# Half of x laid out by feature and loaded first over two queues, in a two-layer decoder trunk

## The chip, the core and the metric

The kernel runs on one core of one Trainium2 chip. The metric is the device time of one execution in microseconds (us), the median of several runs. The engines are named as the profile names them: PE (TensorE, the matrix engine; PEld is its weight load), ACT (ScalarE), DVE (VectorE), POOL (GpSimd) and SP (SyncE, which here only issues DMAs).

## What is computed

A trunk of two pre-norm residual layers with 256 positions and a width of 2048, in float32. Layer 0 is sliding-window attention with sinks, layer 1 attention in three branches. Each layer takes `h = rmsnorm(x)`, projects it (`h @ w_in`), attends, multiplies by a SiLU gate, projects again (`@ w_out`) and adds the result to x. A last rmsnorm ends it. What matters here is the start of layer 0:

```python
def rmsnorm(x, g):
    y = xf * lax.rsqrt(jnp.mean(xf * xf, axis=-1, keepdims=True) + NORM_EPS)
    return (y * g.astype(jnp.float32)).astype(x.dtype)
...
proj = h @ w_in
q, k, v, z = jnp.split(proj, ...)
q = apply_rope(q..., cos, sin); k = apply_rope(k..., cos, sin)
```

The cosines and sines come from `positions`, an input of 256 integers.

## The kernel before

To keep float32 precision in the products, each weight tile and each activation tile is split into a high part (`w_hi`, `hT[...,0,:]`, a rounded copy made on ACT) and a low part (the rest, a subtraction on DVE), and three products per K-tile (high x high, low x high, high x low) go into one PSUM bank. A K-tile is 128 of the 2048 features; there are 16, and the 256 positions are two halves t of 128 rows.

The work is a list of steps. A step loads 512 KB of weights into a tile `raw` (four buffers; `load`), splits it (`split`, three buffers of `w_hi` and `w_lo`; steps 0 and 1 in two halves) and runs its products (`half(0)` for t = 0, `half(1)` for t = 1, six products of 512 columns each). Eight steps fill two of three accumulator banks (`acc`); then `post` evacuates them. The first eight steps are the key and value columns of layer 0, called the first block below; its `post_kv` scales by `r = 1/rms`, which so is needed only there, copies k on ACT and v on DVE, and turns k by the rope tables on POOL.

The products need x by feature: `hT_pair(0, hT0, j)` transposes K-tiles 2j and 2j+1 on PE (four transposes), copies them times the norm's weight `gT` to the high part (ACT) and makes the low part (DVE). Pair 0 comes before the first step, and step i makes pair i+1. `first_block` (line 861) also computes, in steps 4 to 7, the squares of x, 512 columns at a time (`square`, on ACT with a running sum), and in step 7 `scales(0)`: a sum and two small operations on DVE, a power on POOL, then rq and rh on DVE, and `scale_rows`, which spreads rh over the columns with two transposes (`rbc`).

Loads are issued in this order on SP (lines 380 to 390 and 1283 to 1290): the identity matrix with the rope frequencies (`cst`), the norm weights (`nw`), x columns 0 to 511 (two halves), raw[0], x columns 512 to 1023, raw[1], the rest of x between raw[2] and raw[3]. POOL's software queue loads the positions and the sinks. PE bridges the wait with nine products of zeros (`idle`). The norm weights are transposed on PE (`nwT`) to get `gT`; the rope tables are made at once on DVE and ACT.

No instruction runs where it stands in the text. Every operation is recorded (line 217 is the one line that all of them show in the profile), with a price from `_price` (line 160 on). `Plan.order` (line 247) then runs a simulation with these prices: an engine that is free takes, of the operations that can start, the one with the lowest number, where the splits are moved ahead of everything and the products behind everything:

```python
heapq.heappush(able[e], (i - ops[i].early, i))
...
dma_free = max(dma_free, end + 700) + op.bytes / self.BYTES_NS
```

The result is a fixed order for each engine, which the chip follows first in, first out. An entry in `op.order` only forces this order in the plan; an entry in `op.deps` is a real dependence. In the plan a DMA issue costs SP and ACT 60 ns, a dependence into PE has 800 ns of slack, and a power on POOL costs some 500 ns.

Of the kernel before, what the change touches and what calls it, by code (L numbers as in the profile page):

```python
# [163 lines left out]
def _price(eng, method, args, kw, out, ins):  # L164
# [12 lines left out]
    if method == "dma_start":  # L177
        return (1050 if eng == "POOL" else 60, 2200)
    ptrs = sum(isinstance(kw.get(k), View) for k in ("scale", "bias", "scalar", "scalar1"))
# [159 lines left out]
@with_exitstack  # L339
def trunk(ctx: ExitStack, tc: tile.TileContext, x, positions, norm_w, final_norm_w,  # L340
          a_w_in, a_sinks, a_w_out, b_w_in, kc_pos, kc_w1, kc_w2, vc_pos, vc_w1, vc_w2,
          b_w_out, consts, out):
    nc = tc.nc
# [16 lines left out]
    def dram(ap, off, pattern):  # L360
        return bass.AP(tensor=ap.tensor, offset=ap.offset + off, ap=pattern)

    def copy(out, in_, scale=1.0):
        ACT.activation(out, in_, AF.Copy, scale=scale)

# [6 lines left out]
    ps = s_bank("idle")  # L372
    for _ in range(9):
        PE.matmul(ps, idle[:, 0:P], idle, start=True, stop=True)


    pos_i = sb.tile([P, NT], I32, name="pos_i")
    POOL.dma_start(pos_i, dram(positions, 0, [[1, P], [P, NT]]))
    cst = sb.tile([P, P + 8], F32, name="cst")
    SP.dma_start(cst, dram(consts, 0, [[CW, P], [1, P + 8]]))  # L380
    ident = cst[:, 0:P]
    nw = sb.tile([32, 512], F32, tag="q32", name="nw", bufs=2)[:, 0:P]
    SP.dma_start(nw, dram(norm_w, 0, [[P, 32], [1, P]]))
    xt = [sb.tile([P, D], F32, name=f"x{t}") for t in range(NT)]

    def load_x(j):
        for t in range(NT):
            SP.dma_start(xt[t][:, j * NB:(j + 1) * NB], dram(x, t * P * D + j * NB, [[D, P], [1, NB]]))

    load_x(0)  # L390
    sinks = sb.tile([P, 32], F32, name="sinks")
    POOL.dma_start(sinks, dram(a_sinks, 0, [[0, P], [1, 32]]))

    identr = sb.tile([P, P], F32R, name="identr")
    DVE.tensor_copy(identr, ident)
    nhalf = sb.tile([P, 1], F32, name="nhalf")
    DVE.memset(nhalf, -0.5)


    posf = sb.tile([P, NT], F32, name="posf")  # L400
    DVE.tensor_copy(posf, pos_i)
    ang = sb.tile([P, NT, 8], F32, name="ang")
    for t in range(NT):
        DVE.tensor_scalar(ang[:, t], cst[:, P:P + 8], posf[:, t:t + 1], None, op0=OP.mult)
    red = sb.tile([P, 2, NT, 8], F32, name="red")
    rnd = sb.tile([P, 2, NT, 8], F32, name="rnd")
    for i, shift in enumerate((0.0, 0.25)):
        DVE.tensor_scalar(rnd[:, i], ang, 1.0 / (2.0 * math.pi), shift, op0=OP.mult, op1=OP.add)
        DVE.tensor_scalar(rnd[:, i], rnd[:, i], MAGIC, None, op0=OP.add)
        DVE.tensor_scalar(rnd[:, i], rnd[:, i], -MAGIC, None, op0=OP.add)  # L410
        src = ang
        for c in TWO_PI:
            DVE.scalar_tensor_tensor(red[:, i], rnd[:, i], -c, src, op0=OP.mult, op1=OP.add)
            src = red[:, i]
        if i:
            DVE.tensor_scalar(red[:, i], red[:, i], math.pi / 2, None, op0=OP.add)
    lim = float(np.nextafter(np.float32(math.pi), np.float32(0)))
    DVE.tensor_scalar(red, red, lim, -lim, op0=OP.min, op1=OP.max)
    cs = sb.tile([P, NT, 2, 8], F32, name="cs")
    sn = sb.tile([P, NT, 2, 8], F32, name="sn")  # L420
    ACT.activation(sn[:, :, 1, :], red[:, 0], AF.Sin)
    ACT.activation(cs[:, :, 0, :], red[:, 1], AF.Sin)
    DVE.tensor_copy(cs[:, :, 1, :], cs[:, :, 0, :])
    DVE.tensor_scalar(sn[:, :, 0, :], sn[:, :, 1, :], -1.0, None, op0=OP.mult)

# [21 lines left out]
    mflat = mask.rearrange("p a b -> p (a b)")  # L447
    nsink = sb.tile([P, 32], F32, name="nsink")
    DVE.tensor_scalar(nsink, sinks, -1.0, None, op0=OP.mult)

    gT = sb.tile([P, 32], F32, name="gT")
    tb = t_bank("nwT")
    PE.transpose(tb[:, 0, 0:32], nw, ident[0:32, 0:32])
    copy(gT, tb[:, 0, 0:32])


# [66 lines left out]
    def hT_pair(i, hT, j):  # L523

        tb = t_bank("xT")
        for k in range(2):
            for t in range(NT):
                PE.transpose(tb[:, 2 * k + t, :], xt[t][:, (2 * j + k) * P:(2 * j + k + 1) * P], ident)
        src = [tb[:, 2 * k:2 * k + 2, :].rearrange("p a b -> p (a b)") for k in range(2)]
        g = [gT[:, i * KT + 2 * j + k:i * KT + 2 * j + k + 1] for k in range(2)]  # L530
        hi = [hT[:, 2 * j + k, 0, :] for k in range(2)]
        for k in range(2):
            copy(hi[k], src[k], scale=g[k])
        for k in range(2):
            DVE.scalar_tensor_tensor(hT[:, 2 * j + k, 1, :], src[k], g[k], hi[k].bitcast(F32),
                                     op0=OP.mult, op1=OP.subtract)
# [324 lines left out]
    def first_block(i):  # L861
        if i not in first_done:
# [431 lines left out]
    for i, st in enumerate(steps):  # L1294
# [23 lines left out]
def _consts():  # L1318
# [10 lines left out]
    for g in range(NG):  # L1329
# [25 lines left out]
```

## Time and profile before

| | |
|---|---|
| median of 3 runs | 793.22 us (792.34 to 793.55) |
| the profiled execution | 793.6 us, of which its span (first to last instruction) 791.5 |
| mean granted clock of PE | 0.99 |
| busy: PE, DVE, ACT, POOL | 775.1, 562.3, 466.0, 122.9 us |
| DMA | 128.77 MB, mean 163 GB/s |

Busy times of PE are modelled at their ends, so a busy PE is not always PE at its peak. The granted clock is 1.00 at 2.4 GHz and 0.50 at 1.2 GHz. In a timeline, a row is one instruction or several alike in a row; in the chain of waits, each piece is followed back from the last instruction to what released it.

### The profile page before, as it was taken

The page shows a single profiled execution, that of the slowest core. Times are in us where ns is not written, and L with a number is a line of the kernel's source. Part 1 is how long each engine was busy: PE and PEld are TensorE (multiplying, and loading weights), DVE is VectorE, ACT ScalarE, POOL GpSimd, SP SyncE. Part 2 cuts the span into 40 slices and gives each one's busy share as a digit, 9 for nine tenths or more (in the row PEclk, how much of TensorE's full clock was granted, in tenths as well). Part 3 has the DMA queues.
Part 4 walks back from the last instruction along what each step waited for, and adds up shares of the span by engine and source line. Part 5 has one row for each costly group of instructions (what it writes and reads, how often), then busy time and mean ns, then how long its engine had stood idle before and what let it go on. Part 6 is the DMA issues. An engine that isn't in the chain of part 4 may idle for free.

```text
span 791.5 us, 11613 instructions
## 1 busy us (share of the span) xinstructions
PE 775.1 (98%) x4004; PEld 625.8 (79%) x4004; DVE 562.3 (71%) x1164; ACT 466.0 (59%) x941; POOL 122.9 (16%) x169
## 2 busy tenths in 40 slices
PE   7999999999999999999999999999999999999995
PEld 4888878788788788888878887777868768768884
DVE  5657959859779655556756479869949878965562
ACT  6646647557466445554746477567648657744452
POOL 2102311213023000020101021111121131111110
PEclk7999999999999999999999999999999999999998
DMA  8555454554553555565667654434434453354652
GB/s 275 183 186 159 136 186 133 185 161 139 168 173 133 186 185 184 182 191 176 192 216 221 182 160 123 144 109 133 133 107 123 147 147 117 108 186 162 196 174 107
DMA packets 85995, 128.77 MB, mean 163 GB/s; under 512 B 6178, under 2 KB 43265, under 8 KB 85808
## 3 DMA queue, kind: packets, MB, share of 16 engines
q1 hardware_dynamic: 85536, 126.72, 50.5%
q0 software_dynamic: 400, 1.30, 0.6%
q8 instruction: 32, 0.52, 0.3%
q14 instruction: 27, 0.22, 0.1%
HBM read 125.91 MB, written 2.10 MB: 162 GB/s over the span
## 4 chain that ended last, share of the span: by engine, by line
PE 88%; DVE 5%; issue 3%; ACT 1%; DMA 1%; POOL 1%; SPq 0%; ACTq 0%; POOLq 0%; DVEq 0%
PE acc L217 72%; PE pv L217 5%; PE s L217 4%; PE pT L217 4%; DVE sm L217 2%; DVE w_lo L217 1%; PE qT L217 1%; PE xT L217 1%; DMA raw<-in_a_w_in 1%; DVE u L217 1%; ACT w_hi L217 1%; PE gates L217 1%; PE pcT L217 0%; POOL rope L217 0%; PE mlp L217 0%
## 5 line engine op out<-in xcount | busy, mean ns | idle before, releaser
L217 DVE TENSOR_TENSOR w_lo<-raw,w_hi 128x1024 fp32r<-128x1024 f32 (+1 forms) x231 | 293.1, 1271 | 166.0 <-ACT w_hi L217 160.5
L217 ACT ACTIVATE w_hi<-raw 128x1024 fp32r<-128x1024 f32 (+1 forms) x231 | 241.5, 1049 | 193.5 <-PE acc L217 157.3
L217 PE MATMUL acc<-w_hi,hT 128*128 128x512 f32 x768 | 247.1, 398 | 1.1 <-ACT w_hi L217 0.6
L217 PE MATMUL acc<-hT,w_hi 128*128 128x512 f32 x512 | 186.1, 398 | 0.0
L217 PEld LDWEIGHTS acc<-w_hi,hT 128*128 128x128 f32 x768 | 142.6, 190 | 33.4 <-ACT w_hi L217 3.5
L217 PE MATMUL acc<-w_lo,hT 128*128 128x512 f32 x384 | 151.9, 396 | 0.0
L217 PE MATMUL acc<-hT,w_lo 128*128 128x256 f32 x512 | 145.0, 285 | 0.0
L217 PEld LDWEIGHTS acc<-hT,w_hi 128*128 128x128 f32 x512 | 96.2, 188 | 21.9 <-issue 4.1
L217 PEld LDWEIGHTS acc<-hT,w_lo 128*128 128x128 f32 x512 | 96.7, 189 | 1.5 <-issue 0.8
L217 PE MATMUL acc<-w_hi,aT_lo 128*128 128x512 f32 x236 | 92.4, 391 | 0.0
L217 PE MATMUL acc<-w_hi,aT_hi 128*128 128x512 f32 x236 | 92.1, 392 | 0.0
L217 PE MATMUL acc<-w_lo,aT_hi 128*128 128x512 f32 x236 | 92.0, 391 | 0.0
L217 PEld LDWEIGHTS acc<-w_lo,hT 128*128 128x128 f32 x384 | 72.7, 189 | 16.4 <-issue 2.4
L217 ACT ACTIVATE sm<-sm,nmb 128x128 f32<-128x128 f32 (+1 forms) x128 | 56.8, 445 | 17.9 <-DVE nmb L217 15.7
L217 PEld LDWEIGHTS acc<-w_lo,aT_hi 128*128 128x128 f32 x236 | 44.3, 188 | 11.3 <-issue 2.4
L217 PEld LDWEIGHTS acc<-w_hi,aT_hi 128*128 128x128 f32 x236 | 44.3, 188 | 9.7 <-ACT w_hi L217 0.8
L217 PEld LDWEIGHTS acc<-w_hi,aT_lo 128*128 128x128 f32 x236 | 44.3, 188 | 8.9
L217 POOL TENSOR_TENSOR sm<-sm,denb 128x512 f32<-128x512 f32 (+1 forms) x16 | 29.1, 1818 | 140.7 <-DVE denb L217 82.0
L217 DVE CUSTOM_DVE_ANT_0 sm<-s,mask 128x128 f32<-128x128 f32 (+1 forms) x128 | 43.6, 348 | 9.2 <-PE s L217 8.9
L217 PEld LDWEIGHTS pT<-cst,sm 128*128 128x128 f32 x256 | 30.0, 140 | 13.8 <-issue 5.4
L217 PE MATMUL pT<-cst,sm 128*128 128x128 f32 x256 | 38.8, 276 | 1.2 <-DVE sm L217 0.8
L217 PE MATMUL s<-kTB,qT 128*128 128x272 f32 x192 | 37.8, 292 | 0.0
(187 smaller groups left out, 862.3 us busy)
## 6 DMA issues: line engine op xcount, KB each, us to landing
raw<-in_b_w_in SPq DMA_DIRECT2D x88, 512.0 KB, 3.6
raw<-in_a_w_in SPq DMA_DIRECT2D x72, 512.0 KB, 3.5
raw<-in_a_w_out SPq DMA_DIRECT2D x32, 512.0 KB, 3.5
raw<-in_b_w_out SPq DMA_DIRECT2D x32, 512.0 KB, 4.3
x<-in_x SPq DMA_DIRECT2D x8, 256.0 KB, 6.9
raw<-in_b_cmp_k_w SPq DMA_DIRECT2D x4, 512.0 KB, 3.7
raw<-in_b_cmp_v_w SPq DMA_DIRECT2D x4, 512.0 KB, 4.0
out<-x SPq DMA_DIRECT2D x4, 512.0 KB, 3.5
```

Of the source, the lines that this page charges most:

```text
L217: return getattr(eng.real, method)(*[real(a) for a in args], **{k: real(a) for k, a in kw.items()})
```

## The change

Two inputs are new, made on the host: `small` (128 x 74: the norm weights by feature, the sinks, the positions and the rope frequencies, spread over the partitions) and `xT` (K-tiles 0 to 7 of x by feature, 1 MB, so that two K-tiles are 2 KB in a row for each partition). Of x nothing is dropped: it is still loaded whole, but later. ACT issues the loads of `small` and of raw[0], in two halves of 256 KB; SP issues xT, two K-tiles at a time, three loads ahead of raw[1] and the fourth behind it. Pairs 0 to 3 read xT (`xf`) and need no transposes. x columns 1024 to 1535 are loaded ahead of raw[4], then 1536 to 2047 behind raw[4], 0 to 511 behind raw[5], 512 to 1023 behind raw[6]. The squares follow this order of columns, each pair behind a split in the plan; the rope tables and nsink stand in step 5. POOL makes the identity, and issues no load at the start. There is one idle product more, and an issue costs 450 ns in the plan. The core of the diff:

```diff
--- before.py
+++ after.py
...
             return (max(n, 256) / 2.4 + 2, 0)
         return (n * (4 if out.shape[0] > 64 else 2) / 2.4 + 2, 0)
     if method == "dma_start":
-        return (1050 if eng == "POOL" else 60, 2200)
+        return (1050 if eng == "POOL" else 450, 2200)
     ptrs = sum(isinstance(kw.get(k), View) for k in ("scale", "bias", "scalar", "scalar1"))
     ptrs += sum(isinstance(a, View) and math.prod(a.shape[1:]) == 1 and n > 2 for a in args[1:])
     psum = any(v.base.psum for v in ins)
...
     idle = sb.tile([P, NB], BF16, name="idle")
...
     DVE.memset(warm, 0.0)
     ACT.activation(warm, warm, AF.Sin)
     ps = s_bank("idle")
-    for _ in range(9):
+    for _ in range(10):
         PE.matmul(ps, idle[:, 0:P], idle, start=True, stop=True)
-    pos_i = sb.tile([P, NT], I32, name="pos_i")
-    POOL.dma_start(pos_i, dram(positions, 0, [[1, P], [P, NT]]))
-    cst = sb.tile([P, P + 8], F32, name="cst")
-    SP.dma_start(cst, dram(consts, 0, [[CW, P], [1, P + 8]]))
-    ident = cst[:, 0:P]
-    nw = sb.tile([32, 512], F32, tag="q32", name="nw", bufs=2)[:, 0:P]
-    SP.dma_start(nw, dram(norm_w, 0, [[P, 32], [1, P]]))
+    small_t = sb.tile([P, SMALL], F32, name="small")
+    ACT.dma_start(small_t, small)
+    gT = small_t[:, 0:32]
+    sinks = small_t[:, 32:64]
+    pos_i = small_t[:, 64:66].bitcast(I32)
+    inv_freq = small_t[:, 66:74]
     xt = [sb.tile([P, D], F32, name=f"x{t}") for t in range(NT)]
-    def load_x(j):
+    xf = sb.tile([P, KT, S], F32, tag="aT_hi", name="xf")
+    def load_x(j, later=None):
         for t in range(NT):
-            SP.dma_start(xt[t][:, j * NB:(j + 1) * NB], dram(x, t * P * D + j * NB, [[D, P], [1, NB]]))
-    load_x(0)
-    sinks = sb.tile([P, 32], F32, name="sinks")
-    POOL.dma_start(sinks, dram(a_sinks, 0, [[0, P], [1, 32]]))
+            op = SP.dma_start(xt[t][:, j * NB:(j + 1) * NB], dram(x, t * P * D + j * NB, [[D, P], [1, NB]]))
+            if later:
+                op.order.add(later.i)
+    def load_xf(k0, k1):
+        SP.dma_start(xf[:, k0:k1, :], dram(xT, k0 * S, [[XT * S, P], [S, k1 - k0], [1, S]]))
+    for k in range(0, 6, 2):
+        load_xf(k, k + 2)
+    ident = sb.tile([P, P], F32, name="ident")
+    POOL.memset(ident, 1.0)
+    for sign in (1, -1):
+        POOL.affine_select(out=ident, in_=ident, pattern=[[-sign, P]], compare_op=OP.is_ge, fill=0.0,
+                           base=0, channel_multiplier=sign)
     identr = sb.tile([P, P], F32R, name="identr")
     DVE.tensor_copy(identr, ident)
     nhalf = sb.tile([P, 1], F32, name="nhalf")
     DVE.memset(nhalf, -0.5)
...
     cs = sb.tile([P, NT, 2, 8], F32, name="cs")
     sn = sb.tile([P, NT, 2, 8], F32, name="sn")
+    def rope_tables(later):
+        DVE.tensor_scalar(nsink, sinks, -1.0, None, op0=OP.mult).order.add(later.i)
+        posf = sb.tile([P, NT], F32, name="posf")
+        DVE.tensor_copy(posf, pos_i).order.add(later.i)
...
         POOL.affine_select(out=mask_c[:, t], in_=mask_c[:, t], pattern=[[-16, 16]],
                            compare_op=OP.is_ge, fill=NEG, base=P * t - 31, channel_multiplier=1)
     mflat = mask.rearrange("p a b -> p (a b)")
-    nsink = sb.tile([P, 32], F32, name="nsink")
-    DVE.tensor_scalar(nsink, sinks, -1.0, None, op0=OP.mult)
-    gT = sb.tile([P, 32], F32, name="gT")
-    tb = t_bank("nwT")
-    PE.transpose(tb[:, 0, 0:32], nw, ident[0:32, 0:32])
-    copy(gT, tb[:, 0, 0:32])
     urgent, queue = deque(), deque()
     state = {"credit": 0.0, "rate": 0.0}
...
     def square(i, t, j):
         junk = sb.tile([P, NB], F32, tag="q32", name="junk", bufs=2)
-        ACT.activation(junk, xt[t][:, j * NB:(j + 1) * NB], AF.Square, accum_out=ssq[i][:, t, j:j + 1])
+        return ACT.activation(junk, xt[t][:, j * NB:(j + 1) * NB], AF.Square, accum_out=ssq[i][:, t, j:j + 1])
     def rstd(i, ts=slice(0, NT)):
         ms = sb.tile([P, NT], F32, tag="ms", name="ms", bufs=2)[:, ts]
...
     def hT_pair(i, hT, j):
-        tb = t_bank("xT")
-        for k in range(2):
-            for t in range(NT):
-                PE.transpose(tb[:, 2 * k + t, :], xt[t][:, (2 * j + k) * P:(2 * j + k + 1) * P], ident)
-        src = [tb[:, 2 * k:2 * k + 2, :].rearrange("p a b -> p (a b)") for k in range(2)]
+        if i == 0 and 2 * j < XT:
+            src = [xf[:, 2 * j + k, :] for k in range(2)]
+        else:
+            tb = t_bank("xT")
+            for k in range(2):
+                for t in range(NT):
+                    PE.transpose(tb[:, 2 * k + t, :], xt[t][:, (2 * j + k) * P:(2 * j + k + 1) * P], ident)
+            src = [tb[:, 2 * k:2 * k + 2, :].rearrange("p a b -> p (a b)") for k in range(2)]
         g = [gT[:, i * KT + 2 * j + k:i * KT + 2 * j + k + 1] for k in range(2)]
         hi = [hT[:, 2 * j + k, 0, :] for k in range(2)]
         for k in range(2):
...
     def load(st):
         raw = sb.tile([P, 1024], F32, tag="raw", name="raw", bufs=4)
         st.raw = raw
-        st.dma(raw)
+        if st.idx == 0:
+            for k in range(2):
+                ACT.dma_start(raw[:, k * NB:(k + 1) * NB],
+                              dram(a_w_in[0], k * P * A_IN + 2048, [[A_IN, P], [1, NB]]))
+            return
+        st.load = st.dma(raw)
     def split(st):
         n = st.cols
...
         parts = 2 if st.idx < 2 else 1
         for c in range(parts):
             part = slice(c * n // parts, (c + 1) * n // parts)
-            copy(st.hi[:, part], st.raw[:, part])
-            DVE.tensor_sub(st.lo[:, part], st.raw[:, part], st.hi[:, part])
+            st.ops = (copy(st.hi[:, part], st.raw[:, part]),
+                      DVE.tensor_sub(st.lo[:, part], st.raw[:, part], st.hi[:, part]))
         plan.early = 0
     def w_dma(w, row0, nk, col0, ncol, width):
         def dma(raw):
-            SP.dma_start(raw[:, 0:nk * ncol].rearrange("p (k n) -> p k n", k=nk),
+            return SP.dma_start(raw[:, 0:nk * ncol].rearrange("p (k n) -> p k n", k=nk),
                          dram(w, row0 * width + col0, [[width, P], [P * width, nk], [1, ncol]]))
         return dma
...
                 hT_pair(0, hT0, i + 1)
             if i >= 4:
                 for t in range(NT):
-                    square(0, t, i - 4)
+                    square(0, t, (i - 2) % 4).order.add(steps[i + 1].ops[0].i)
+            if i == 5:
+                rope_tables(steps[i + 1].ops[1])
             if i == KT // 2 - 1:
                 scales(0)
                 scale_rows(0)
...
     AHEAD, LOADS = 2, 4
     for i, st in enumerate(steps):
         st.idx = i
-    for i in range(min(LOADS, n)):
+    load(steps[0])
+    for i in range(1, LOADS):
         load(steps[i])
-        if i + 1 < 4:
-            load_x(i + 1)
+        if i == 1:
+            load_xf(6, 8)
     hT_pair(0, hT0, 0)
     for i in range(AHEAD):
         split(steps[i])
...
             mlp_loads()
         if i == nA + 8:
             queue.append(pipeline(units, b_front, b_back))
+        if i == 0:
+            load_x(2)
         if i + LOADS < n:
             load(steps[i + LOADS])
+        if i < 3:
+            load_x((i + 3) % 4, steps[i + LOADS].load)
         if i + AHEAD < n:
             split(steps[i + AHEAD])
         for h in st.halves[:1] if i >= n - KT // 2 else st.halves:
...
+XT = 8
+SMALL = 74
+def _small(norm_w, a_sinks, positions):
+    parts = [norm_w.reshape(-1, P).T, np.broadcast_to(a_sinks.reshape(1, -1), (P, 32)),
+             np.ascontiguousarray(positions.reshape(NT, P).T).view(np.float32),
+             np.broadcast_to(np.asarray(INV_FREQ, np.float32), (P, 8))]
+    return np.ascontiguousarray(np.concatenate([np.ascontiguousarray(a) for a in parts], axis=1))
...
+    data["small"] = _small(*(np.asarray(inputs[name]) for name in ("norm_w", "a_sinks", "positions")))
+    data["xT"] = np.ascontiguousarray(data["x"].reshape(S, KT, P)[:, :XT].transpose(2, 1, 0).reshape(P, XT * S))
```

## Rows read from the trace of the kernel before

**Rows 1.** The page, busy times of engines, and the granted clock in 40 slices.

```profile
PE 775.1 (98%) x4004; PEld 625.8 (79%) x4004; DVE 562.3 (71%) x1164; ACT 466.0 (59%) x941; POOL 122.9 (16%) x169
...
PEclk7999999999999999999999999999999999999998
```

**Rows 2.** Windows, the long stretch: start:end, length, busy by engine, clock, DMA.

```profile
20.00:780.00 760.00, 757.01 (x3945) 613.86 (x3944) 549.74 (x1121) 451.26 (x906) 118.25 (x152) 1.00 0.51 161
```

**Rows 3.** Windows of the start; the last columns are PEclk, DMA share, GB/s.

```profile
core 0: us, PE busy (x) PEld busy (x) DVE busy (x) ACT busy (x) POOL busy (x), PEclk, DMA share, GB/s
1.50:3.50 2.00, 2.00 (x6) 0.75 (x5) 0.25 (x1) 0.78 (x2) 1.99 (x5) 1.00 0.51 155
3.50:7.00 3.50, 1.89 (x8) 0.59 (x6) 0.78 (x7) 0.81 (x3) 1.77 (x8) 1.00 0.81 114
7.50:18.00 10.50, 9.09 (x27) 6.80 (x28) 7.32 (x21) 9.74 (x25) 0.00 (x0) 0.51 1.05 393
9.95:17.80 7.85, 7.34 (x20) 5.46 (x21) 5.87 (x11) 7.57 (x19) 0.00 (x0) 0.50 1.05 389
17.80:38.95 21.15, 21.15 (x104) 17.51 (x102) 13.86 (x24) 12.42 (x23) 2.34 (x4) 1.00 0.60 196
```

**Rows 4.** Timeline of PE at the start: start us, us, instructions.

```profile
1.25 3.52 PE L217 MATMUL idle<-idle 128*128 128x512 bf16 x9 [1.25 <-DVE warm L217]
...
3.78 0.99 PE L217 MATMUL idle<-idle 128*128 128x512 bf16 x3
...
5.31 0.44 PE L217 MATMUL xT<-cst,x 128*128 128x128 f32 x2 [0.36 <-DMA x<-in_x]
7.79 1.54 PE L217 MATMUL xT<-cst,x 128*128 128x128 f32 x6 [2.05 <-DMA x<-in_x]
9.95 1.22 PE L217 MATMUL acc<-w_hi,hT 128*128 128x512 f32 x2 [0.62 <-ACT w_hi L217]
```

**Rows 5.** Chain of waits up to 42 us: start us, us, what.

```profile
2.64 6.61 DMA raw<-in_a_w_in
...
27.07 0.44 PE xT L217 x4
...
29.36 0.22 PE rbc L217 x2
29.58 12.26 PE acc L217 x54
```

**Rows 6.** DMA queues from 3.5 to 7 us, and issues up to 5 us.

```profile
q1 hardware_dynamic: 215, 0.38, 44.6%
q0 software_dynamic: 57, 0.02, 36.8%
...
cst<-in_consts SPq DMA_DIRECT2D x1, 68.0 KB, 1.9
...
pos_i<-in_positions POOLq DMA_DIRECT2D x1, 1.0 KB, 4.8
sinks<-in_a_sinks POOLq DMA_DIRECT2D x1, 16.0 KB, 5.6
```

**Rows 7.** Groups by shape up to 39 us: busy us, mean ns, idle before.

```profile
L217 ACT ACTIVATE w_hi<-raw 128x1024 fp32r<-128x1024 f32 x9 | 9.5, 1058 | 4.9 <-PE acc L217 4.3 <-DVE vA L217 0.6
L217 ACT ACTIVATE hT<-xT,gT 128x256 fp32r<-128x256 f32 x16 | 6.9, 469 | 3.3 <-PE xT L217 3.3
L217 ACT ACTIVATE junk<-x 128x512 f32<-128x512 f32 x8 | 5.0, 628 | 4.7 <-DMA x<-in_x 4.7
L217 ACT ACTIVATE w_hi<-raw 128x512 fp32r<-128x512 f32 x4 | 2.3, 624 | 0.0
L217 ACT ACTIVATION_READ_ACCUMULATOR junk<-x 128x1 f32 x8 | 1.6, 196 | 0.0
L217 ACT ACT_TABLE_LOAD x1 | 1.3, 1283 | 0.8 <-PEq L1343 0.8
```

**Rows 8.** Timeline: the norm's scale r, and the first evacuation.

```profile
22.93 0.15 DVE L217 TENSOR_REDUCE ms<-ssq 128x2 f32<-128x8 f32 x1
...
23.37 1.79 POOL L217 TENSOR_TENSOR r<-ms,nhalf 128x2 f32<-128x2 f32 x1 [18.10 <-DVE ms L217]
...
37.85 0.47 ACT L217 ACTIVATE k<-acc,r 128x256 f32<-128x256 f32 x1 [0.59 <-PE acc L217]
```

More of the change, by code (lines that the diff above doesn't have):

```diff
@@ L339, in trunk @@
 @with_exitstack
-def trunk(ctx: ExitStack, tc: tile.TileContext, x, positions, norm_w, final_norm_w,
-          a_w_in, a_sinks, a_w_out, b_w_in, kc_pos, kc_w1, kc_w2, vc_pos, vc_w1, vc_w2,
-          b_w_out, consts, out):
+def trunk(ctx: ExitStack, tc: tile.TileContext, x, final_norm_w, a_w_in, a_w_out, b_w_in, kc_pos, kc_w1, kc_w2, vc_pos, vc_w1, vc_w2,
+          b_w_out, consts, small, xT, out):
     nc = tc.nc
@@ L363, in copy @@
     def copy(out, in_, scale=1.0):
-        ACT.activation(out, in_, AF.Copy, scale=scale)
+        return ACT.activation(out, in_, AF.Copy, scale=scale)
     idle = sb.tile([P, NB], BF16, name="idle")
@@ L397, in trunk @@
     DVE.memset(nhalf, -0.5)
-    posf = sb.tile([P, NT], F32, name="posf")
-    DVE.tensor_copy(posf, pos_i)
-    ang = sb.tile([P, NT, 8], F32, name="ang")
-    for t in range(NT):
[L404 to L416, printed above, removed]
@@ L417, in trunk @@
-    lim = float(np.nextafter(np.float32(math.pi), np.float32(0)))
-    DVE.tensor_scalar(red, red, lim, -lim, op0=OP.min, op1=OP.max)
+    nsink = sb.tile([P, 32], F32, name="nsink")
     cs = sb.tile([P, NT, 2, 8], F32, name="cs")
     sn = sb.tile([P, NT, 2, 8], F32, name="sn")
[L421 to L424, printed above, removed]
+    def rope_tables(later):
+        DVE.tensor_scalar(nsink, sinks, -1.0, None, op0=OP.mult).order.add(later.i)
+        posf = sb.tile([P, NT], F32, name="posf")
+        DVE.tensor_copy(posf, pos_i).order.add(later.i)
+        ang = sb.tile([P, NT, 8], F32, name="ang")
+        for t in range(NT):
+            DVE.tensor_scalar(ang[:, t], inv_freq, posf[:, t:t + 1], None, op0=OP.mult)
+        red = sb.tile([P, 2, NT, 8], F32, name="red")
+        rnd = sb.tile([P, 2, NT, 8], F32, name="rnd")
+        for i, shift in enumerate((0.0, 0.25)):
+            DVE.tensor_scalar(rnd[:, i], ang, 1.0 / (2.0 * math.pi), shift, op0=OP.mult, op1=OP.add)
+        DVE.tensor_scalar(rnd, rnd, MAGIC, None, op0=OP.add)
+        DVE.tensor_scalar(rnd, rnd, -MAGIC, None, op0=OP.add)
+        src = ang[:, None].to_broadcast([P, 2, NT, 8])
+        for c in TWO_PI:
+            DVE.scalar_tensor_tensor(red, rnd, -c, src, op0=OP.mult, op1=OP.add)
+            src = red
+        DVE.tensor_scalar(red[:, 1], red[:, 1], math.pi / 2, None, op0=OP.add)
+        lim = float(np.nextafter(np.float32(math.pi), np.float32(0)))
+        DVE.tensor_scalar(red, red, lim, -lim, op0=OP.min, op1=OP.max)
+        ACT.activation(sn[:, :, 1, :], red[:, 0], AF.Sin)
+        ACT.activation(cs[:, :, 0, :], red[:, 1], AF.Sin)
+        DVE.tensor_copy(cs[:, :, 1, :], cs[:, :, 0, :])
+        DVE.tensor_scalar(sn[:, :, 0, :], sn[:, :, 1, :], -1.0, None, op0=OP.mult)
@@ L523, in hT_pair @@
     def hT_pair(i, hT, j):
-        tb = t_bank("xT")
-        for k in range(2):
-            for t in range(NT):
-                PE.transpose(tb[:, 2 * k + t, :], xt[t][:, (2 * j + k) * P:(2 * j + k + 1) * P], ident)
-        src = [tb[:, 2 * k:2 * k + 2, :].rearrange("p a b -> p (a b)") for k in range(2)]
+        if i == 0 and 2 * j < XT:
[3 more added lines that the diff above has]
+            for k in range(2):
+                for t in range(NT):
+                    PE.transpose(tb[:, 2 * k + t, :], xt[t][:, (2 * j + k) * P:(2 * j + k + 1) * P], ident)
+            src = [tb[:, 2 * k:2 * k + 2, :].rearrange("p a b -> p (a b)") for k in range(2)]
         g = [gT[:, i * KT + 2 * j + k:i * KT + 2 * j + k + 1] for k in range(2)]
@@ L1332, in _consts @@
     return c
-_INS = ["x", "positions", "norm_w", "final_norm_w", "a_w_in", "a_sinks", "a_w_out", "b_w_in",
+XT = 8
[5 more added lines that the diff above has]
+    return np.ascontiguousarray(np.concatenate([np.ascontiguousarray(a) for a in parts], axis=1))
+_INS = ["x", "final_norm_w", "a_w_in", "a_w_out", "b_w_in",
         "b_cmp_k_pos", "b_cmp_k_w1", "b_cmp_k_w2", "b_cmp_v_pos", "b_cmp_v_w1", "b_cmp_v_w2", "b_w_out"]
```

## The prediction

> **What bounds the kernel now.** I read the page first. TensorE (PE) is busy for 775.1 of 791.5 us [rows 1], so the time is PE's work plus the time in which PE is idle or slow. The granted clock says where: its slices stand at 7, then 9, to the last. The stretch from 20 to 780 us holds 757.0 us of PE work in 760.0 [rows 2]: only 3.0 us are free there, so whatever the first 20 us give back is carried to the end. DVE, at 549.7 us in that stretch, has room.
>
> Then I cut the start into stretches [rows 3] and put PE's instructions beside them [rows 4]. PE runs nine idle products from 1.25 us, a few transposes of x as x lands, and its first product of weights at 9.95. The chain of waits names what it waited for: the first weight tile raw, issued at 2.64, takes 6.61 us [rows 5]. From 9.95 to 17.80 the clock is 0.50 (1.2 GHz); from 17.80 to 38.95, where the first block (96 products of the key/value columns) ends, it is 1.00 and PE is never idle [rows 3]. At 37.85 ACT begins to evacuate the block's first bank, at 38.95 its last product is done.
>
> Why do the first tiles land late? Between 3.5 and 7.0 us all 16 DMA engines together move 114 GB/s, from 7.5 on 393 [rows 3]. In that slow stretch the software queue, the one that POOL feeds, takes 36.8% of the engines for 0.02 MB, the hardware queue 44.6% [rows 6]. Its two transfers, positions and sinks, land 4.8 and 5.6 us after their issue, together 17 KB; when they are gone the rate is full. I read this as cause, though the overlap in time is all that the rows show.
>
> **The change, part by part.** I follow two marks: the first product (9.95 us) and the end of the first block (38.95).
>
> First product. Gone are POOL's two transfers, the transfers of cst and nw, and the transposes of nw and of the first pair. It now needs small (128 x 74 numbers, 37 KB), two K-tiles of xT (256 KB) and half of raw[0] (256 KB). The nearest small transfer, cst with 68 KB, landed 1.9 us after its issue at 0.80 [rows 6]. At 393 GB/s, bytes moving from about 1.8 us, 549 KB take 1.4 us and would be there at 3.2; if all three xT loads that SP issues at once (768 KB) share the engines with ACT's queue, 1,061 KB take 2.8 us, up to 4.6. With some 0.5 us to completion that is 3.7 to 5.1. Then come a half copy of raw (0.62 us) and a copy of xT (0.47) on ACT [rows 7]: 4.8 to 6.2. PE is not free before either: ten idle products, nine of which reach 4.77, end at about 5.0 [rows 4]. ACT's table load, 1.28 us [rows 7], may stand in front of its DMA issues or between the two halves of raw[0]; in the first case everything is 1.3 us later, 7.5 at worst. I take 5.7: a gain of 4.25.
>
> First the row on the queues: with one hardware queue in use, the engines already reach 393 GB/s [rows 3], so no row here has a second queue adding rate. The Trainium skill (DMA: Bandwidth & Descriptors, Rules for kernel authors) says that spreading transfers over SP, ACT and GpSimd does not help bandwidth, since they share the 16 engines and interleave; by that, the second queue gives only issue time, and raw[0] shares with xT loads that nobody needs yet: the first product at the late end, 6.2, and a time 0.5 us above my sum.
>
> First block, first product to end. Before: 29.0 us, of which 21.15 run at full clock and 7.85 at half, 0.51 of these idle [rows 3]. Its content at full pace: 96 products at 0.227 us (54 take 12.26) make 21.8; seven groups of four transposes at 0.44 make 3.1; the two of rbc 0.22 [rows 5]: 25.1. So 29.0 - 25.1 = 3.9 us went to the half clock and the waits, 0.5 and 3.4. After: four groups of transposes remain (pairs 4 to 7; the first pair's four lay ahead of 9.95), 1.76 us, so 1.3 us go; the content is 21.8 + 1.8 + 0.2 = 23.8. Does the clock stay up? The first six idle products take the 2.53 us from 1.25 to 3.78, 0.42 each, the last three 0.99 together [rows 4]: PE came to 2.4 GHz there, and is at half clock after it had nothing to do from 5.75 to 7.79. With products from 5.7 on, that hole is gone. I leave 1.2 us for waits (0.5 as before for hT's low part, 0.7 for the second half of raw[0], issued after the table load); bounds 0 and the 3.9 of before. End of the block: 5.7 + 23.8 + 1.2 = 30.7, against 38.95: **8.25 us earlier**.
>
> Later loads. Until raw[1] has landed 1,829 KB must move: at 393 GB/s 4.8 us, so near 7.1; step 1 begins at 5.7 + 1.2 + 2.7 = 9.6. Each further step takes PE 2.7 us and DMA 1.3 (512 KB). The 1 MB of xT more costs 2.7 us of DMA that no one waits for. On SP, x's loads now stand behind raw[4], raw[5] and raw[6], which wait for a split to free a buffer; x0 and x1 then land by 20 or so. Their squares come after the split of step 8, which starts about 24.
>
> Squares (eight at 0.63 us plus a read of 0.19) [rows 7] leave ACT's start and stand in steps 4 to 7, where ACT has 1.06 + 0.94 + 1.64 = 3.6 us a step against PE's 3.2; but it is not loaded in steps 0 to 3, and splits go first in the order. Free until r is late: last squares at about 26.2, two DVE operations and POOL's power (1.79 us) [rows 8] give r near 28.8. The first bank is full at 29.3, and a third bank covers PE for 1.4 us after the block's end. So nothing is paid, with some 2 us to spare. What would be next in line is rbc's transposes: if PE's queue has them before r is there, PE stands with all products behind them; up to 1 us, which I keep for the range.
>
> Rope tables, nsink: ten to fifteen DVE operations of about 0.2 us in steps 5 to 7, hidden by DVE's room; first used by POOL after r. The identity made on POOL, not loaded: ready before 5 us, needed first by pair 4. xf lives in aT_hi's room, which is written long after. The price of 450 for an issue moves the planner's order only; I set it at 0 and give it 1 us either way, from the 3.0 us that PE is free in the long stretch [rows 2].
>
> **Sum.** 793.6 (profiled execution, 2.1 us above its span) - 8.2 = 785.4; it stands 0.4 above the median of the runs, so 785.0 us.
>
> **The rivals.**
> *The start of the DMA is slow for another reason.* For it: the two queues only overlap in time. Against it: the rate rises as the last of POOL's transfers lands. Then 0.71 MB have moved by 7.0 us (155 GB/s for 2.0 us, 114 for 3.5) [rows 3], raw[1] lands at 7.0 + 1.16 MB / 393 GB/s + 0.5 = 10.5, step 1 starts near 11.1, and seven steps with their transposes (21.0) end at 32.1: gain 6.8, **786.4 us**.
> *The clock falls all the same*, because the first product is late or the first step has holes: the 3.4 us of half clock come back, **788.4 us**. For it: the clock stayed low from 7.5 to 17.8 although PE was busy 9.1 of 10.5 us [rows 3]. Against it: the low pace began after a real hole.
> *No change*: a later stage swallows the gain. DVE would have to be the bound; PE's 757.0 of 760.0 speaks against it. **793.2 us**.
> *Slower: r comes last and holds the banks.* Place: the scale of the key/value evacuation. r is needed by about 31.6 (third bank full at 32.1, less ACT's 0.47 [rows 8]). Each us later is paid in full by PE. It decides against the kernel from a delay of 8.2 + 1.6 = 9.8 us, r at 41.4: x1's load would have to be held behind a raw buffer for 12 us more than I count. With r at 43.4: **795.0 us**.
>
> **How the numbers follow.** My forecast 0.60, slow DMA 0.15, half clock 0.17, no change 0.04, slower 0.04. 0.2% (1.6 us) is about what a measurement can tell from no change. All of the first three cases are faster: 0.92; the same 0.04; slower 0.04. The range: with no waits and the first product at 5.0 the block ends at 28.8, a gain of 10.1, 783.1, and with 0.5 us for the order 782.6. Above: half clock and 1 us of order or rbc, 789.4. Outside are the last two cases and some of the ends.
>
> **What would show it.** The rate between 3.5 and 7 us near 390 GB/s with no software queue; first product at 5 to 6.2 us; clock 1.00 from the idle products on, with no 0.50 stretch; four groups of transposes in the first block; the first ACT evacuation at 29 to 30.5 us instead of 37.85; from there every mark some 8 us earlier to the end. It would be wrong if a 0.50 stretch stands after 7 us, if PE waits for r or rbc near 28, or if PE's free time between 20 and 780 us grows beyond 4 us.

## The result, and the profile after

The changed kernel takes 786.38 us (median of 4 runs, 786.12 to 786.83) against 793.01 of the kernel before (4 runs): 6.63 us less, a ratio of 0.9918 with a 95% interval of 0.9906 to 0.9930. I had predicted 785.0, in a range of 782.6 to 789.4. The profiled execution takes 786.12 us, its span 784.4.

First the stretches that answer to [rows 3] and [rows 2]. Windows of the changed kernel; the last columns are the granted clock, the DMA share and GB/s:

```profile
core 0: us, PE busy (x) PEld busy (x) DVE busy (x) ACT busy (x) POOL busy (x), PEclk, DMA share, GB/s
1.50:3.50 2.00, 2.00 (x6) 0.74 (x5) 0.55 (x2) 1.49 (x2) 1.98 (x10) 1.00 0.54 120
3.50:7.00 3.50, 2.40 (x7) 0.67 (x6) 1.09 (x3) 1.77 (x4) 0.44 (x3) 1.00 0.99 357
7.50:18.00 10.50, 10.04 (x49) 7.99 (x48) 7.78 (x13) 7.97 (x16) 0.00 (x0) 1.00 1.05 389
6.81:31.10 24.29, 23.83 (x112) 19.44 (x113) 19.54 (x42) 20.19 (x43) 0.00 (x0) 1.00 0.96 338
```

From 3.5 to 7 us DMA moves 357 GB/s where it moved 114. But from 1.5 to 3.5 it moves 120, less than the 155 of before. From 7.5 to 18 us the clock is 1.00 where it was 0.51, and PE works on 49 instructions there instead of 27.

PE's start, against [rows 4], in the timeline of the changed kernel:

```profile
1.26 4.45 PE L217 MATMUL idle<-idle 128*128 128x512 bf16 x10 [1.26 <-DVE warm L217]
6.81 1.20 PE L217 MATMUL acc<-w_hi,hT 128*128 128x512 f32 x4 [1.10 <-ACT w_hi L217]
7.85 0.63 PE L217 MATMUL acc<-w_lo,hT 128*128 128x512 f32 x2
8.93 1.20 PE L217 MATMUL acc<-w_hi,hT 128*128 128x512 f32 x4 [0.46 <-ACT w_hi L217]
...
10.43 1.07 PE L217 MATMUL acc<-w_hi,hT 128*128 128x512 f32 x4
```

The first product comes at 6.81 us instead of 9.95. It waits 1.10 us for ACT's copy, and the products of the second K-tile another 0.46. The thirteenth product starts at 10.43, a mark that is used below. The chain of waits says why, against [rows 5]:

```profile
1.24 4.87 DMA raw<-in_a_w_in
...
6.13 0.63 ACT w_hi L217
6.76 1.60 ACT hT L217 x4
8.36 0.53 ACT w_hi L217
...
8.93 5.29 PE acc L217 x22
```

The first half of raw[0] lands 4.87 us after its issue. The second half lands near 7.8, and on ACT four copies of xT stand ahead of its copy, until 8.36. From 8.93 on the chain is PE's alone. The transfers, against [rows 6] (queues from 3.5 to 7 us, then issues up to 5 us):

```profile
q1 hardware_dynamic: 392, 0.72, 58.5%
q10 hardware_dynamic: 333, 0.53, 40.9%
...
xf<-in_xT SPq DMA_DIRECT2D x4, 256.0 KB, 5.1
...
raw<-in_a_w_in ACTq DMA_DIRECT2D x2, 256.0 KB, 5.4
small<-in_small ACTq DMA_DIRECT2D x1, 37.0 KB, 3.9
```

The software queue is gone and ACT's queue (q10) is there. The 37 KB of small need 3.9 us. Late in the block, r and the evacuation, against [rows 8]:

```profile
31.41 0.70 POOL L217 TENSOR_TENSOR r<-ms,nhalf 128x2 f32<-128x2 f32 x1 [27.47 <-DVE ms L217]
...
32.26 0.82 ACT L217 ACTIVATE k<-acc,r 128x256 f32<-128x256 f32 x2
```

r is ready at 32.1, later than the block's end (31.1 us: the window from 6.81 on holds 112 instructions, the block's 96 products and 16 transposes), and yet PE waits for nothing there: it is busy for all of the 20 us from 32 to 52. Is the gain carried to the end? A mark in the middle of layer 1, the weights of its small network, in the kernel before:

```profile
L217 PEld LDWEIGHTS mlp<-w_hi,X x32: 182/183/187, 386.1 to 424.1; 128*122 128x122 f32 x32
```

and after:

```profile
L217 PEld LDWEIGHTS mlp<-w_hi,X x32: 182/183/187, 378.9 to 416.9; 128*122 128x122 f32 x32
```

7.2 us earlier there, and 7.1 at the end of the span.

### The profile page after: what moved, and what is told of

Read it like the earlier page. It is cut to its first block, busy times and chain, and to the rows that moved or that the text cites. A ratio compares the mean times of both kernels' runs of the same rounds, so it can differ in the third digit from the quotient of the medians.

```text
span 784.4 us, 11578 instructions
## 1 busy us (share of the span) xinstructions
PE 769.8 (98%) x3988; PEld 621.3 (79%) x3988; DVE 561.3 (72%) x1159; ACT 465.8 (59%) x940; POOL 121.7 (16%) x170
## 4 chain that ended last, share of the span: by engine, by line
PE 90%; DVE 4%; issue 2%; ACT 1%; DMA 1%; POOL 1%; ACTq 0%; POOLq 0%; DVEq 0%
PE acc L217 74%; PE pv L217 5%; PE s L217 4%; PE pT L217 4%; DVE sm L217 1%; DVE w_lo L217 1%; PE qT L217 1%; ACT w_hi L217 1%; PE xT L217 1%; DMA raw<-in_a_w_in 1%; PE gates L217 1%; DVE u L217 0%; PE pcT L217 0%; POOL rope L217 0%; PE mlp L217 0%
## 5 line engine op out<-in xcount | busy, mean ns | idle before, releaser
L217 PE MATMUL acc<-w_hi,hT 128*128 128x512 f32 x768 | 243.6, 394 | 1.6 <-ACT w_hi L217 1.6
L217 POOL TENSOR_TENSOR sm<-sm,denb 128x512 f32<-128x512 f32 (+1 forms) x16 | 28.8, 1798 | 140.9 <-DVE denb L217 71.4
L217 PEld LDWEIGHTS pT<-ident,sm 128*128 128x128 f32 x256 | 30.0, 140 | 13.7 <-issue 5.4
L217 PE MATMUL pT<-ident,sm 128*128 128x128 f32 x256 | 38.8, 276 | 1.2 <-DVE sm L217 0.8
```

Source lines behind the costliest of these rows:

```text
L217: return getattr(eng.real, method)(*[real(a) for a in args], **{k: real(a) for k, a in kw.items()})
```

## The experiments

Each run is compared with runs of the kernel before on the same chip. The last two columns are its median less theirs, and the ratio with its 95% interval. The change itself is the first line.

| run | median us | less before | ratio |
|---|---|---|---|
| the change | 786.38 | -6.63 | 0.9918 (0.9906 to 0.9930) |
| before, without POOL's loads | 791.95 | -0.78 | 0.9986 (0.9977 to 0.9995) |
| change, with POOL's loads | 787.54 | -5.19 | 0.9931 (0.9918 to 0.9945) |
| change, x by rows | 791.62 | -1.11 | 0.9989 (0.9980 to 0.9998) |
| change, one queue | 785.87 | -6.86 | 0.9913 (0.9899 to 0.9926) |
| change, 4 idle products | 788.06 | -4.71 | 0.9939 (0.9924 to 0.9954) |
| before, 17 idle products | 795.01 | +2.24 | 1.0027 (1.0016 to 1.0038) |
| change, price 60 | 786.54 | -6.23 | 0.9923 (0.9908 to 0.9938) |
| change, late r | 788.96 | -3.81 | 0.9957 (0.9940 to 0.9973) |
| one queue by need | 785.23 | -7.55 | 0.9904 (0.9889 to 0.9919) |
| two queues by need | 787.47 | -5.31 | 0.9926 (0.9914 to 0.9939) |
| change, again | 786.36 | -6.42 | 0.9921 (0.9907 to 0.9934) |
| two queues by need, 14 idle | 786.21 | -6.48 | 0.9919 (0.9905 to 0.9932) |

**POOL's loads, taken from the kernel before.**

```diff
-    pos_i = sb.tile([P, NT], I32, name="pos_i")
-    POOL.dma_start(pos_i, dram(positions, 0, [[1, P], [P, NT]]))
+    small_t = sb.tile([P, SMALL], F32, name="small")
+    ACT.dma_start(small_t, small)
+    sinks = small_t[:, 32:64]
+    pos_i = small_t[:, 64:66].bitcast(I32)
...
-    POOL.dma_start(sinks, dram(a_sinks, 0, [[0, P], [1, 32]]))
```

> The kernel before, with one thing of the change: positions and sinks come with the packed load small (37 KB) on ACT's hardware queue, so POOL's software queue issues nothing at the start; cst, nw, the transposes and x by rows stay. Theory A (POOL's two transfers slow the start of the DMA): between 3.5 and 7 us the rate rises from 114 to over 300 GB/s, raw[0] lands about 2 us earlier (near 7.2 instead of 9.25), and the time falls by 2 to 4 us against the kernel before. Rival B (the start is slow for a reason of its own, and the change wins by needing fewer bytes): the rate stays near 114 GB/s, raw[0] lands within 0.5 us of 9.25, the time within 0.8 us of before.

Window, chain and PE's timeline of this run:

```profile
3.50:7.00 3.50, 3.50 (x14) 1.79 (x12) 2.09 (x18) 1.63 (x7) 0.00 (x0) 1.00 0.85 262
...
2.65 5.35 DMA raw<-in_a_w_in
...
9.58 1.68 PE L217 MATMUL acc<-w_hi,hT 128*128 128x512 f32 x3 [2.46 <-ACT hT L217]
```

The rate more than doubles and raw[0] lands at 8.00 instead of 9.25, so POOL's two loads did slow the start, by less than theory A said (over 300 GB/s, 2 us). The time falls by only 0.78 us, which is what rival B gave. PE waits 2.46 us for a copy of hT, which ACT makes only after the copies of raw[0] (8.02 to 9.07 us): an earlier landing is worth only what the fixed orders of ACT and PE behind it let through.

**POOL's loads, put back into the change.**

```diff
-    sinks = small_t[:, 32:64]
-    pos_i = small_t[:, 64:66].bitcast(I32)
+    pos_i = sb.tile([P, NT], I32, name="pos_i")
+    POOL.dma_start(pos_i, dram(positions, 0, [[1, P], [P, NT]]))
+    sinks = sb.tile([P, 32], F32, name="sinks")
+    POOL.dma_start(sinks, dram(a_sinks, 0, [[0, P], [1, 32]]))
```

> The changed kernel with positions and sinks loaded again over POOL's software queue at the start, as before the change; all else as changed. Theory A: between 3.5 and 7 us the rate falls from 357 GB/s to under 200, the first product moves from 6.81 us to 8 or later, and the time rises by 1.2 us or more. Rival B: rate and first product stay within 10% and 0.4 us, and the time within 0.6 us.

A window, a piece of the chain and PE's timeline of this run:

```profile
3.50:7.00 3.50, 2.35 (x7) 0.62 (x6) 1.38 (x4) 1.74 (x4) 2.67 (x12) 1.00 0.94 292
...
1.81 8.00 DMA raw<-in_a_w_in
...
10.51 1.20 PE L217 MATMUL acc<-w_hi,hT 128*128 128x512 f32 x4 [1.98 <-ACT w_hi L217]
```

About 1.4 us slower than the change (-5.19 against -6.63), as theory A has it in the time, not in the place. The first product stays (6.85 us) and the rate falls only to 292. What comes late is the second half of raw[0], which lands at 9.81 instead of about 7.8: the second K-tile's products start at 10.51 instead of 8.93.

**x by rows.** No xT; columns 0 to 511 and 512 to 1023 of x take the place of its loads, and all pairs are transposed.

```diff
-    for k in range(0, 6, 2):
-        load_xf(k, k + 2)
+    load_x(0)
...
-            load_xf(6, 8)
+            load_x(1)
...
-        if i == 0 and 2 * j < XT:
+        if False:
```

> The changed kernel without xT: all eight pairs are transposed on PE, and x by rows (columns 0 to 511, then 512 to 1023) is loaded at the place of the xT loads and not again later; the two queues, small, the order of the squares stay. From the rows: three groups of transposes at 0.44 us come back on PE (1.3 us), the first pair's four stand ahead of the first product (0.6 to 1.5 us), and 512 KB instead of 256 KB must land first (0.6 us). Theory: 2.0 to 3.4 us slower than the changed kernel. Rival (the layout by feature earns nothing, since PE's transposes fill holes of a DMA-bound start, and 1 MB less is moved): within 0.8 us of it.

PE's timeline and a window of this run:

```profile
7.92 0.73 PE L217 MATMUL acc<-w_hi,hT 128*128 128x512 f32 x2 [0.80 <-ACT hT L217]
11.91 0.58 PE L217 MATMUL acc<-w_hi,hT 128*128 128x512 f32 x1 [3.26 <-DVE hT L217]
...
12.50:15.50 3.00, 3.00 (x12) 2.50 (x12) 2.56 (x5) 1.78 (x3) 0.00 (x0) 0.50 0.99 317
```

5.5 us slower than the change (-1.11 against -6.63): far over my 2.0 to 3.4. The first product is 1.1 us later, where I had counted 1.2 to 2.1, but behind it PE stands for 3.26 us. (The ten executions lie at 791.4 to 791.7 and 792.2 to 792.6 us; the profiled one, 792.44, is one of the upper four.) In DVE's fixed order the low part of hT comes after the low parts of raw[0]'s second half and of raw[1], which land last. Behind that hole the clock is at 0.50 from 12.5 to 15.5 us. I had added up transposes and bytes; what they set off was dearer.

**One queue.** small, xT 0 and 1, raw[0], then the rest, all on SP.

```diff
-    ACT.dma_start(small_t, small)
+    SP.dma_start(small_t, small)
...
-                ACT.dma_start(raw[:, k * NB:(k + 1) * NB],
+                SP.dma_start(raw[:, k * NB:(k + 1) * NB],
```

> The changed kernel with all loads on SP's queue: small, xT K-tiles 0 and 1, the two halves of raw[0], then the other xT loads and raw[1] and so on. Theory (the engines are shared, the second queue only saves issue time; what counts is that nothing unneeded stands ahead): the first product comes at 6.3 to 7.0 us, the time is within 0.6 us of the changed kernel, rather below it. Rival (two queues feed the engines faster at the start): first product 0.8 us or more later than 6.81, the time 0.8 us or more above.

PE's timeline of this run:

```profile
6.40 1.19 PE L217 MATMUL acc<-w_hi,hT 128*128 128x512 f32 x4 [0.70 <-ACT w_hi L217]
...
12.53 1.20 PE L217 MATMUL acc<-w_hi,hT 128*128 128x512 f32 x4 [0.40 <-ACT w_hi L217]
```

The first product is earlier, and the time cannot be told from the change's, as the theory had it. Here small, at the head of one queue, lands 1.9 us after its issue, not 3.9. On ACT's queue it took 2.2 us in the kernel before without POOL's loads, which points to the xT loads beside it in the change and not to the queue. The Trainium skill (DMA: Bandwidth & Descriptors, Rules for kernel authors) says that spreading DMAs over several issuing engines does not help bandwidth. The time agrees. In bytes two queues had moved 1.49 MB by 7.0 us and one queue 1.38, so the second queue did bring some earlier, but not those that the first steps need.

**Four idle products.**

```diff
-    for _ in range(10):
+    for _ in range(4):
```

> The changed kernel with 4 idle products instead of 10, so that PE does nothing from about 3.0 us to the first product of weights near 6.8. Theory (the idle products keep PE's clock up, and half clock costs): the first products run at 0.50 for 3 to 5 us, as they did for 3.7 us in the run with x by rows, and the time rises by 1.2 to 2.5 us against the changed kernel (half of the stretch). Rival (the first steps are fed by DMA and ACT, so PE's pace does not matter there): the clock may fall, but the time stays within 0.6 us.

Timeline and a window:

```profile
1.26 1.89 PE L217 MATMUL idle<-idle 128*128 128x512 bf16 x4 [1.26 <-DVE warm L217]
7.25 2.08 PE L217 MATMUL acc<-w_hi,hT 128*128 128x512 f32 x4 [4.11 <-ACT w_hi L217]
...
12.49 1.09 PE L217 MATMUL acc<-w_hi,hT 128*128 128x512 f32 x4
...
9.00:10.00 1.00, 1.00 (x4) 0.71 (x4) 1.00 (x3) 1.00 (x3) 0.00 (x0) 1.00 1.06 389
```

1.9 us slower than the change, within what the clock theory gave. The first twelve products take the 5.2 us from 7.25 to 12.49, 0.44 each, which is 512 columns at 1.2 GHz; in the change they take 3.6, from 6.81 to 10.43. So half clock costs 1.6 us here, and the rest is a first product that comes 0.4 later. Yet the window shows a granted clock of 1.00. So at the start of a profile that column cannot be read alone; the spacing of the products tells the level.

**More idle products in the kernel before**, 17 instead of 9.

> The kernel before with 17 idle products instead of 9, which reach to between 6.5 and 8.2 us and so fill the hole ahead of x's second half (7.79). Theory (clock): PE stays at 1.00 past 7.7 us; of the 3.4 us that half clock cost before, 1.5 to 3.4 come back. Rival (the first steps wait for weights that land at 12 us and later, so a faster PE only waits more): less than 0.8 us gained, with holes in PE between 10 and 18 us.

PE's timeline of this run:

```profile
10.24 0.66 PE L217 MATMUL xT<-cst,x 128*128 128x128 f32 x4 [2.20 <-ACT gT L217]
13.23 1.68 PE L217 MATMUL acc<-w_hi,hT 128*128 128x512 f32 x3 [2.33 <-ACT hT L217]
```

A miss: 2.24 us slower. The idle products stand in PE's queue ahead of nwT (7.21 us instead of 4.70), and in this plan ACT makes gT only at 10.01, behind the copies of raw[0]; the first product is at 13.23, and the hole ahead of it is only moved. It says nothing on the clock in the kernel before.

**The planner's price**, 60 instead of 450.

```diff
-        return (1050 if eng == "POOL" else 450, 2200)
+        return (1050 if eng == "POOL" else 60, 2200)
```

> The changed kernel with the planner's old price of 60 ns for a DMA issue of SP or ACT; every instruction is the same, only the planned order may differ. Theory: the order moves the time by less than 0.6 us. Rival: the price is a part of the gain, 0.8 us or more slower.

786.54 us, 0.4 above the change by the table and inside the spread of its own executions (785.75 to 787.45): no part of the gain can be seen to lie in the price.

**A late r.**

```diff
+        if i == 0:
+            slow, ones = xf[:, 8:10, :], xf[:, 10:12, :]
+            POOL.memset(ones, 1.0)
+            wide = ms[:, :, None].to_broadcast([P, NT, 256])
+            POOL.tensor_tensor(out=slow, in0=wide, in1=ones, op=OP.mult)
+            for _ in range(2):
+                POOL.tensor_tensor(out=slow, in0=slow, in1=ones, op=OP.mult)
+            ms = xf[:, 8:10, 0]
```

> The changed kernel with three products by one (128x512 each, about 1.8 us) on POOL ahead of the power that gives r in layer 0, so r is ready near 37.5 us instead of 32.1. My prediction counted 1.4 us of cover behind the end of the first block (31.1 us), so every microsecond past 32.5 is paid: 4 to 5 us slower than the changed kernel. Rival (the plan goes on with the first halves of the following steps in the third bank, as long as three buffers of split weights reach, some 4 us): 1 to 2 us slower, or less.

PE's timeline:

```profile
35.44 0.39 PE L217 MATMUL acc<-w_lo,hT 128*128 128x512 f32 x1
37.58 0.40 PE L217 MATMUL rbc<-ident,rh 128*128 128x128 f32 x2 [1.75 <-DVE rh L217]
38.33 0.70 PE L217 MATMUL acc<-w_hi,hT 128*128 128x512 f32 x2 [0.35 <-DVE vA L217]
```

r is ready at 37.2 and costs 2.8 us, between the two. PE works on to 35.8 us, 4.5 us past the block's end rather than my 1.4: the plan runs the first halves of steps 8, 9 and 10 in the third bank, as far as three buffers of split weights reach. Then PE waits for rh, since rbc's transposes are next in its queue.

**The order of need.** One queue: small, xT 0 and 1, raw[0], xT 2 and 3, raw[1], and so on. In the second kernel ACT issues raw[0].

```diff
-    for k in range(0, 6, 2):
-        load_xf(k, k + 2)
+    load_xf(0, 2)
...
     for i in range(1, LOADS):
+        load_xf(2 * i, 2 * i + 2)
         load(steps[i])
-        if i == 1:
-            load_xf(6, 8)
```

> The changed kernel with all loads on SP's queue, in the order in which the steps need them: small, xT 0 and 1, raw[0] in two halves, xT 2 and 3, raw[1], xT 4 and 5, raw[2], xT 6 and 7, raw[3]. In the run with one queue the first product came at 6.40 us and PE waited 0.40 us more at 12.5 us for a weight tile that stood behind two xT loads. Theory (only the order of landing counts): first product near 6.4, no wait at 12.5, 0.3 to 1.0 us faster than the changed kernel. Rival (the start is bound by ACT's copies and not by landings): within 0.3 us of it.

> As the one before, but the two halves of raw[0] are issued by ACT, beside small and xT 0 and 1 on SP, so that the first-needed loads are issued at once and nothing else is beside them. Theory (the second queue only saves issue time, some 0.9 us of two issues): first product between 5.9 and 6.4 us, within 0.4 us of the run with one queue by need, not slower than the changed kernel. Rival (two queues land their loads later, since they share the engines from the start): first product later than 6.6 us, the time as in the changed kernel or above.

> The changed kernel itself, on the same chip as the two before, to compare with: 0.9918 of the kernel before, within its interval.

The changed kernel came back at 786.36 us. Its timeline in this second profile:

```profile
7.04 1.20 PE L217 MATMUL acc<-w_hi,hT 128*128 128x512 f32 x4 [1.51 <-ACT w_hi L217]
...
10.64 1.07 PE L217 MATMUL acc<-w_hi,hT 128*128 128x512 f32 x4
```

of the one queue by need, with a window:

```profile
6.74 1.20 PE L217 MATMUL acc<-w_hi,hT 128*128 128x512 f32 x4 [1.03 <-ACT w_hi L217]
...
9.59 1.07 PE L217 MATMUL acc<-w_hi,hT 128*128 128x512 f32 x4
...
7.50:18.00 10.50, 10.50 (x52) 8.69 (x52) 7.97 (x13) 8.05 (x15) 0.00 (x0) 1.00 1.05 393
```

and of the two queues, with two pieces of the chain of waits:

```profile
1.26 3.80 PE L217 MATMUL idle<-idle 128*128 128x512 bf16 x10 [1.26 <-DVE warm L217]
7.15 1.52 PE L217 MATMUL acc<-w_hi,hT 128*128 128x512 f32 x3 [2.09 <-ACT hT L217]
8.46 0.63 PE L217 MATMUL acc<-w_lo,hT 128*128 128x512 f32 x1
8.89 1.05 PE L217 MATMUL acc<-w_hi,hT 128*128 128x512 f32 x2
...
1.24 4.80 DMA raw<-in_a_w_in
...
6.60 0.50 ACT hT L217
```

One queue by need takes 785.23 us, 1.13 less than the change beside it, and no execution of the one overlaps with one of the other (785.0 to 785.3 against 786.3 to 787.1). That is a little more than the 0.3 to 1.0 that I expected, though the first product is later than the 6.4. The gain lies in the first twelve products: the first comes 0.30 us earlier than in the change beside it, the thirteenth 1.05 (9.59 against 10.64), since the halves of raw[0] land 4.1 and 4.4 us after their issue (4.9 and 6.0 in the change's first profile) and are copied one right behind the other, where in the change four copies of xT stand between. From 7.5 to 18 us PE has no hole. **It beats both kernels.**

Two queues by need is a miss: the time is the rival's, though not by late landings of raw[0]. Its first half is copied early (4.24 us) and its second lands at 6.04, no later than on one queue. But in ACT's fixed order the copies of xT stand behind the copy of this second half, where one queue by need has pair 0's ahead of both: they begin at 6.60, and the first product comes at 7.15. The executions fall in two groups: 785.91 and 785.99, then 787.47 to 787.75. The profiled one is of the slower group. Its ten idle products took 3.80 us, so PE was idle from 5.06 to 7.15, and the first products run at the half-clock spacing of 0.43 us. The faster group has no profile; its mean granted clock over the execution is 0.996, that of the slower 0.994.

**Fourteen idle products** in the kernel with two queues by need.

```diff
-    for _ in range(10):
+    for _ in range(14):
```

> The kernel with two queues by need, with 14 idle products instead of 10. Its five executions fell in two groups, 785.9 to 786.0 and 787.5 to 787.8 us; the profiled one is of the upper group, and there the idle products ended at 5.06 us, ahead of a hole of 2.1 us, and the first products ran at 0.43 us each. Theory (the groups are the clock falling in that hole or not): 14 idle products end between 5.7 and 7.3 us, the hole is closed or short, and all executions lie in or below the lower group, at 786.2 or less. Rival (the groups come from when the loads land): both groups remain, some executions above 787.2.

PE's timeline of this run:

```profile
1.26 4.95 PE L217 MATMUL idle<-idle 128*128 128x512 bf16 x14 [1.26 <-DVE warm L217]
7.07 0.50 PE L217 MATMUL acc<-w_hi,hT 128*128 128x512 f32 x1 [0.86 <-ACT hT L217]
...
8.36 0.62 PE L217 MATMUL acc<-w_hi,hT 128*128 128x512 f32 x2
8.83 0.40 PE L217 MATMUL acc<-w_lo,hT 128*128 128x512 f32 x1
```

All five executions lie between 786.10 and 786.32 us (up to 0.1 over the 786.2 that I expected): the slower group is gone, and from 8.13 us on the products follow each other at 0.23 us. So the groups were the clock, at half or full behind the hole, and half clock at the start costs some 1.6 us (787.6 against 786.0), as with four idle products.

## Why the prediction was right, and where not

**The bound** held: PE has no hole from 8.93 us to the block's end, and of the 7.6 us gained there (38.95 less 0.22 for rbc, which now comes later, against 31.1) 7.2 are there in layer 1 and 7.1 at the end. No later stage swallowed it: from 20 us to 772.9, the same distance from the end as 780 before, PE is free for 2.9 us (3.0 before, and I had set 4 as the sign of being wrong). The price of the planner, which I had set at 0, is 0 within the runs.

**First product: mis-sized.** I took 5.7 us, 4.25 earlier; it is 6.81 (7.04 in the second profile), 3.14 earlier, outside my 4.8 to 6.2. The step that failed is "at 393 GB/s, bytes moving from about 1.8 us": the first half of raw[0] lands at 6.11, not by 5.1 at the latest, since from 1.5 to 3.5 us the engines move 120 GB/s, without any load of POOL. The rival of a DMA start that is slow for another reason was true for these two microseconds, my own theory for the time from 3.5 to 7 us (114 to 262 GB/s in the kernel before, when only POOL's loads go). And small took 3.9 us with three xT loads beside it, not the 1.9 of cst; at the head of a single queue it takes 1.9. Two terms cost less than I gave them: ACT's table load delayed no issue (raw[0]'s second half was issued at 1.79 us), and xT's copy was done before raw[0] landed. The 0.5 us to completion in my sum is shown by no run; the profile gives the time from issue to landing as one, 4.87 us for that half. The sentence on two queues gave the better number (6.2).

**First block: right in size, in part by luck.** I gave 23.8 us of content and 1.2 of waits, 25.0; it took 24.3, with 0.46 of waits. The clock stayed up, but my reason, that the hole ahead of the first product would be gone, came true only in part: PE was idle for 1.1 us there (1.5 in the second profile) and kept its clock. With 2.1 and 4.1 us of idleness, in the runs with two queues by need and with four idle products, it did not. The rival's price was too high: half clock costs 1.6 us, not 3.4. With four idle products it covers twelve products and 5.2 us, not the 7.85 of before, and at full clock these twelve take 3.6 us, of which 0.9 is waiting.

**r: wrong in the step, without effect by luck.** I had it at 28.8, needed by 31.6; it was ready at 32.1, and the first evacuation began at 32.26, not at 29 to 30.5. The squares came later on ACT, between the splits (the last ends at 30.2, not 26.2). By my own terms this had to cost time. It cost none because the other term was wrong too: PE has work for 4.5 us past the block's end, not 1.4, as the run with the late r shows. That rival's price is also mis-added: r at 43.4 is 11.8 us past 31.6 and by its own rule gives 796.8, not 795.0.

**The parts.** I gave the layout by feature 1.3 us for the transposes and a share of the first product. The run with x by rows shows 5.5 us: without it PE stands behind a fixed order of DVE and loses the clock besides. POOL's loads, which stood first in my argument, are worth 0.8 us in the kernel before and about 1.4 in the changed one. The second queue gains nothing, and in the order of need it costs 0.7 us even in the faster group (785.95 against 785.23). The parts don't add up, since the gain of each goes through the same first product and the same clock.

**The size.** My number is 1.4 us too low. Half of it is in the profiled execution, 786.1 where my sum gives 785.4: the block ends 0.6 us later than I said (1.1 for the first product, less 0.5 in the block, rbc left out), another 0.5 of the gain is lost between there and the end, which no row here locates, and 0.4 comes back since 1.7 us instead of 2.1 lie outside the span. The other half is spread: I set the median 0.4 below the profiled execution, and it lies 0.3 above.

What stays open: why the engines move only 120 to 155 GB/s from 1.5 to 3.5 us in the two kernels. With raw[0] at the head of ACT's queue and small with xT on SP (both kernels with two queues by need) they move 219 and 213, in the other runs 112 to 150. So the order of issue matters there, but no run tells which part of it does.

## What to carry to other kernels

Where the main engine is busy to the end, a shorter start is worth its full length, but measure it as the time of the first product and of the last hole behind it, not as bytes. Load in the order in which the first steps need things; a second queue with unneeded loads beside it made the needed ones late, and a fixed order of copies can give away what an early landing gains. Let idle products reach to the first real one: where they ended 2.1 us ahead of it, three executions of five were 1.6 us slower, and that looks like noise until the two groups are seen.

## What was not expected of the hardware

The granted clock is shown as 1.00 at the start although the products run at the spacing of 1.2 GHz (0.44 us for 512 columns, with four idle products); with two queues by need it does show it, 0.57 from 7.15 to 11.02 us. The moment at which the clock rises within the idle products moves between executions: ten of them took 4.45 and 4.26 us in two executions of the changed kernel, and 3.80 with two queues by need. The Trainium skill (TensorE: Matmul & The Clock Gate, Part 1: The HAM clock gate) says that the throttled state is the default and activity lifts it; the twelve slow products after four idle ones agree. And the same power on POOL, 128x2, at the first block's end, took 1.72 to 1.79 us in the three profiles with the start of the kernel before and 0.70 to 0.72 in the eleven of the changed one; why is open, and spans on POOL are rough.
